# A two-layer Conformer-style trunk: the FFN's feature tiles in parts of 4, 9 and 9 instead of 5, 8 and 9, with two of GpSimd's weight sums in other buffers

## The chip, the cores and the metric

The kernel runs on one core of a Trainium2 chip. The metric is the device time of one execution in microseconds; before the change its median over three runs is 1799.12 us (1798.94 to 1799.37). The engines of the core go by their profile names: PE (TensorE, matrix products), DVE (VectorE), ACT (ScalarE), POOL (GpSimd) and SP (SyncE, which here only issues DMAs). Each engine works through its own queue in order and waits on semaphores for what other engines and DMAs have to finish first.

## The reference

The trunk has two layers on one sequence of 512 positions with 1024 channels. Only the FFNs matter for the change; there are four of them, two in each layer, before and after a mixer of convolution and differential attention.

```python
def swiglu(h, w_gate, w_up, w_down):
    return (jax.nn.silu(h @ w_gate) * (h @ w_up)) @ w_down
...
    for l in range(DEPTH):
        x = x + 0.5 * swiglu(rms_norm(x, ffn1_norm[l]), ffn1_w_gate[l], ffn1_w_up[l], ffn1_w_down[l])
        h = rms_norm(x, mix_norm[l])
...
        x = x + jnp.concatenate([conv_out, diff_out], axis=-1) @ w_out[l]
        x = x + 0.5 * swiglu(rms_norm(x, ffn2_norm[l]), ffn2_w_gate[l], ffn2_w_up[l], ffn2_w_down[l])
```

All of it is float32. `w_gate` and `w_up` are 1024 x 2816, `w_down` is 2816 x 1024. The mixer also needs one scalar lambda per layer (exponentials of two sums of products) and a table of relative-position biases; both depend on small inputs alone and are made once.

## The kernel before

**Products in three parts.** The activation `x` lies in SBUF with channels on the partitions, as 8 tiles of 128 x 512. Each float32 operand of a large product is split into a high part (ACT, L96) and a low part (DVE, L97, the value minus its high part), and a product is three matmuls: high by high, high by low, low by high (L159, L162, L163 in `mm3`). `ring` hands out the buffers for weights: `wraw` has 5 slots of 128 x 1024 for weights as loaded, `whi` and `wlo` have 4 each for the parts.

**FFN.** `ffn` works on the 22 feature tiles (128 features each) in three parts, `PARTS = ((0, 5), (5, 8), (13, 9))`: first tile and number of tiles of each. For each part it makes the gated activations of its tiles (`hh`, `hl`, high and low), then the down projection of this part (`ps_d`, L455 to L463), whose result DVE adds to `x` by one eviction for each of the eight output tiles m (L463). A down projection is three matmuls of 128x512 for each pair of feature tile and m, so 24 per feature tile. `gather` (L103) loads its weights on SP, eight blocks of 128 columns at a time.

There are two ways to make a feature tile's gate and up products:

- Plain tiles, those below `PLAIN`, which is the number of tiles in the first part. Each is 2 x 8 x 3 = 48 matmuls of 128x512 (`products`). DVE and ACT then multiply by the norm's factors, apply SiLU and gate (L441 to L444), and split the result (L407). The norm's factors `r` come from statistics that are made while the first tiles are multiplied, so these products work on unnormalized `x`.
- Seven-product tiles, all others. `seven` treats gate and up as the two halves of one 2 x 2 block product and does it with seven block products in place of eight, each of 4 x 3 matmuls of 128x256: 84 (L367). It needs sums of blocks on both sides. Those of the activation are made once for each FFN, after `r` is known, by `Halves`: DVE normalizes `x` into `hn` (L326), makes the differences in `ht` (L330 to L333), ACT and DVE split these into `th` and `tl` (L335), and `settle` splits `hn` itself into `acth` and `actl` (L341) after the part's last plain product, in the buffers that held the unnormalized parts.

**Sums of weights.** `sums` (L120) makes those of the weights for each seven-product tile. SP loads the gate block (`whole`, one `wraw` slot), halves of gate and up into a second slot (`two`), and a third of 128 x 512 in `wraw2`. A DMA from POOL's queue adds half of the up block to both halves of `two` (L137). POOL then makes two more sums (L142, L143) in a third `wraw` slot, `more`. ACT and DVE split all seven operands.

**PSUM.** `turn_tag` deals three pairs of banks in turn, to each feature tile's two banks (`pair_banks`) and to each two outputs m of a down projection; a bank is reused when whoever read it last is done. `tmp` is a pool of scratch buffers, where the norms keep squares (`sq`, two), their sum (`ssum`, one) and a diagonal (`diag`, one).

**Work on the side.** `aside`, passed to the first FFN of layer 0 alone, calls `make_scalars` (lambda: a load on POOL's queue and products on POOL, L496 and L498; a sum on DVE, L500) and `make_bias` (the bias table: one-hot loads, a small matmul `ps_bias` L480, negation on DVE L481, and DMAs through DRAM on POOL's queue, L477, L482, L484). They are called where the tile loop comes to m = 4. A scheduler orders the instructions of each engine from there on; some matmuls are held to their place in the program by `keep_in_program_order`.

Of the kernel before, what the change touches and what calls it, by code (L numbers as in the profile page):

```python
# [11 lines left out]
F32 = mybir.dt.float32  # L12
# [3 lines left out]
ALU = mybir.AluOpType  # L16
AX = mybir.AxisListType

P = 128
DEPTH = 2  # L20
SEQ = 512
# [4 lines left out]
FT = DFF // P  # L26
# [14 lines left out]
HS = SEQ // 2  # L41


PARTS = ((0, 5), (5, 8), (13, 9))
PLAIN = PARTS[0][1]

SPACE = 392
# [19 lines left out]
def trunk(ctx: ExitStack, tc: tile.TileContext, xt, par, lamv, relb, onehot,  # L67
          gu1, dn1, wag, wqkv, wout, gu2, dn2, out):
    nc = tc.nc
    V, S, G, T = nc.vector, nc.scalar, nc.gpsimd, nc.tensor  # L70
# [5 lines left out]
    tmp = ctx.enter_context(tc.tile_pool(name="tmp", bufs=2))  # L76
# [3 lines left out]
    def f32(ap):  # L80
        return ap.bitcast(F32)
# [9 lines left out]
    def ring(tag, n=1024):  # L91
        dt = F32 if "raw" in tag else F32R
        return wp.tile([P, n], dt, tag=tag, name=tag, bufs=RING[tag])

    def parts_of(raw, hi, lo, eng=None):
        S.activation(hi, raw, AF.Copy)  # L96
        (eng or V).tensor_tensor(out=lo, in0=raw, in1=f32(hi), op=ALU.subtract)  # L97

    def chunk(src, eng=None):
        raw, hi, lo = ring("wraw"), ring("whi"), ring("wlo")  # L100
        nc.sync.dma_start(raw, src)
        parts_of(raw, hi, lo, eng)
        return hi, lo  # L103

    def gather(src, blocks, eng=None):
# [11 lines left out]
        parts_of(raw[:, c], hi[:, c], lo[:, c], eng)  # L117
        return hi, lo

    def sums(g, u):  # L120

        h = slice(0, 512), slice(512, 1024)
        w = {}

        def give(name, t, n, raw):
            w[name] = tuple(p[:, h[n]] for p in t)
            parts_of(raw, *w[name])

        whole = ring("wraw")
        nc.sync.dma_start(whole, g)  # L130
        two = ring("wraw")
        nc.sync.dma_start(two[:, h[0]], g[:, h[0]])
        nc.sync.dma_start(two[:, h[1]], u[:, h[1]])
        u2 = ring("wraw2", 512)
        nc.sync.dma_start(u2, u[:, h[1]])

        nc.gpsimd.dma_start(  # L137
            two.rearrange("p (b c) -> p b c", b=2), u[:, h[0]].unsqueeze(1).broadcast_to([P, 2, 512]), accum_op=ALU.add
        )

        more = ring("wraw")
        G.tensor_tensor(more[:, h[0]], two[:, h[1]], whole[:, h[0]], op=ALU.add)  # L142
        G.tensor_tensor(more[:, h[1]], more[:, h[0]], whole[:, h[1]], op=ALU.add)  # L143
        t = ring("whi"), ring("wlo")
        parts_of(whole, *t)
        for n, name in enumerate(("g1", "g2")):
            w[name] = tuple(p[:, h[n]] for p in t)
        t = ring("whi"), ring("wlo")
        give("u2u1", t, 0, two[:, h[1]])
        give("g1u2u1", t, 1, more[:, h[0]])  # L150
        give("u2", (ring("whi2", 512), ring("wlo2", 512)), 0, u2)
        t = ring("whi"), ring("wlo")
        give("all", t, 0, more[:, h[1]])
        give("g1u1", t, 1, two[:, h[0]])
        return w

# [21 lines left out]
    for half in range(2):  # L178
        h, kk = slice(half * 512, (half + 1) * 512), range(half * KT // 2, (half + 1) * KT // 2)
# [88 lines left out]
    def products(pr, w, ps, i, at=None, amid=None):  # L268

        got = None  # L270
        for k in range(KT):
            if k == at:
                got = amid()
            mm3(ps, wpart(w[i], k), pr[k], k == 0, k == KT - 1, pin=at is not None and k in (0, at))
        return got

    def lead_products(pr, w, ps):

        for k in range(KT):
            for n in range(2):  # L280
                for i in range(2):
                    mm3(ps[n][i], wpart(w[n][i], k), pr[k], k == 0, k == KT - 1)
        return rows_rstd(pr.s, DM, pin=True)[0]

    def first_products(pr, w, ps, early=False):


        if not early:
            rc, v = rows_rstd(pr.s, DM)
            r = spread(rc, "rb", split=True)  # L290
        for k in range(KT):
            if early and k == STATS_AT:
                rc, v = rows_rstd(pr.s, DM, pin=True)
            for i in range(2):
                mm3(ps[0][i], wpart(w[0][i], k), pr[k], k == 0, k == KT - 1, pin=early and k in (0, STATS_AT))
        for i in range(2):
            for k in range(KT):
                if early and i == 0 and k == STATS_AT:
                    r = spread(rc, "rb", pin=True)
                mm3(ps[1][i], wpart(w[1][i], k), pr[k], k == 0, k == KT - 1, pin=early and k in (0, STATS_AT))  # L300
        return rc, v, r
# [4 lines left out]
    def pair_banks(turn):  # L306
        tag = turn_tag(turn)
        return [bank(tag, "ps_pair") for _ in range(2)]
# [88 lines left out]
    def ffn(pr, gu, dn, after, lead=None, aside=None):  # L397
        with tc.tile_pool(name="ffn", bufs=1) as fp:
            r = halves = None
            for m0, many in PARTS:  # L400
                hh, held, late = [], [], []

                def gated(n, us):
                    hi = fp.tile([P, SEQ], F32R, tag=f"hh{n}", name="hh")
                    lo = fp.tile([P, SEQ], F32R, tag=f"hl{n}", name="hl")
                    S.activation(hi, us, AF.Copy)
                    V.tensor_tensor(lo, us, f32(hi), op=ALU.subtract)  # L407
                    hh.append((hi, lo))

                def finish():  # L410
                    if late:
                        n, rest = late.pop()
                        gated(n, rest())

                for mm in range(many):
                    m = m0 + mm
                    if m == 4 and aside:
                        aside()
                    if m >= PLAIN:
                        w = sums(gu[m, 0], gu[m, 1])  # L420
                        late.append((mm, seven(halves, w, pair_banks(m), fp, finish, mm == many - 1)))
                        continue
                    w = lead[m] if lead and m < 2 else [chunk(gu[m, 0]), chunk(gu[m, 1])]
                    held.append((mm, w, pair_banks(m)))
                    if m == 0:
                        continue
                    if m == 1 and lead:
                        rc = lead_products(pr, [h[1] for h in held], [h[2] for h in held])
                        continue
                    if m == 1:  # L430
                        _, _, r = first_products(pr, [h[1] for h in held], [h[2] for h in held])
                    elif r is None:
                        products(pr, w, held[-1][2][0], 0)
                        r = products(pr, w, held[-1][2][1], 1, 3, lambda: spread(rc, "rb", pin=True, split=True))
                    else:
                        for i in range(2):
                            products(pr, w, held[-1][2][i], i)
                    for n, _, ps in held:
                        gs = fp.tile([P, 2, SEQ], F32, tag="gn", name="gs", bufs=2)
                        us = gs[:, 1]  # L440
                        V.tensor_tensor(gs[:, 0], ps[0], r, op=ALU.mult)  # L441
                        S.activation(gs[:, 0], gs[:, 0], AF.Silu)
                        V.tensor_tensor(us, ps[1], r, op=ALU.mult)
                        V.tensor_tensor(us, us, gs[:, 0], op=ALU.mult)  # L444
                        gated(n, us)
                    held = []
                    if not halves:
                        halves = Halves(fp, pr, r)
                finish()
                if m0 == 0:  # L450
                    halves.settle()
                blocks = [divmod(m0 + kk, HALF) for kk in range(many)]
                blocks = [(half, m * HALF + f) for m in range(KT) for half, f in blocks]
                w = None
                for m in range(KT):  # L455

                    ps = bank(turn_tag(m0 + many + m // 2), "ps_d")
                    for kk in range(many):
                        b = m * many + kk
                        if b % 8 == 0:  # L460
                            w = gather(dn, blocks[b : b + 8])
                        mm3(ps, wpart(w, b % 8), hh[kk], kk == 0, kk == many - 1)
                    V.scalar_tensor_tensor(x[:, m, :], ps, 0.5, x[:, m, :], op0=ALU.mult, op1=ALU.add)  # L463
                    if m0 + many == FT:
                        after(m)
# [354 lines left out]
    def aside():  # L820
        make_scalars()
        make_bias()
# [92 lines left out]
```

## Time and profile before

| | |
|---|---|
| median of 3 runs | 1799.12 us (1798.94 to 1799.37) |
| profiled execution, time | 1801.19 us |
| profiled execution, span | 1799.4 us |
| PE busy | 1782.5 us, 99%, 10836 matmuls |
| DVE busy | 1225.8 us, 68%, 1858 instructions |
| ACT busy | 895.1 us, 50% |
| POOL busy | 644.3 us, 36%, 460 instructions |
| granted PE clock | 1.0 |

The span runs from the first to the last instruction of the profiled execution. A busy share is a mean over the whole span, while each stage has its own limit, so the times below are read from windows and timelines of single stages. Matmuls are pipelined and the profile draws each longer than its pitch; the pitch is the distance of two starts. The row of a timeline gives start, duration, engine, line and operation, output and inputs, and in brackets how long the engine had been idle and what ended that. Rows with a count of x2 or more are several instructions in succession.

### The profile page before, as it was taken

The numbers are of one execution on the slowest core, as the hardware profiler recorded it, in microseconds if no ns is written. First come the engines' busy times: TensorE is split into PE (matmuls) and PEld (weight loads), VectorE is DVE, ScalarE is ACT, GpSimd is POOL, SyncE is SP. The second block draws the span as 40 slices with busy tenths as digits, with TensorE's granted clock in tenths as the row PEclk, the third lists the DMA queues.
The fourth block names the chain that finished last, engine by engine and source line by source line (L and its number), as shares of the span: only waits on it lengthen the run. The fifth ranks groups of instructions, "written<-read, shape, count | busy, mean of one in ns | idle before, by whom it ended". The sixth has DMA issues, their size and how long they took to land.

```text
span 1799.4 us, 28320 instructions
## 1 busy us (share of the span) xinstructions
PE 1782.5 (99%) x10836; PEld 1588.6 (88%) x10836; DVE 1225.8 (68%) x1858; ACT 895.1 (50%) x1478; POOL 644.3 (36%) x460
## 2 busy tenths in 40 slices
PE   8999999999999999999999999999999999999999
PEld 6899899888778899899888998998887888998997
DVE  7966477568867867477567764765788587674762
ACT  5555255445854446256333653654558354552651
POOL 4242132269943132133112422312797332322320
PEclk9999999999999999999999999999999999999999
DMA  7366467333212266466333654663231133664651
GB/s 242 104 177 187 103 162 199 105 106 93 71 44 87 85 165 184 115 166 183 115 96 94 170 170 108 187 181 118 70 108 57 48 103 92 164 181 112 181 148 59
DMA packets 111145, 231.24 MB, mean 129 GB/s; under 512 B 12087, under 2 KB 32326, under 8 KB 111008
## 3 DMA queue, kind: packets, MB, share of 16 engines
q1 hardware_dynamic: 90912, 191.93, 32.8%
q0 software_dynamic: 19808, 37.33, 12.4%
q8 instruction: 85, 1.39, 0.3%
q14 instruction: 52, 0.43, 0.1%
q10 hardware_dynamic: 288, 0.16, 0.0%
HBM read 227.26 MB, written 3.42 MB: 128 GB/s over the span
## 4 chain that ended last, share of the span: by engine, by line
PE 92%; DVE 2%; DMA 2%; issue 1%; ACT 1%; POOL 0%; POOLq 0%; SPq 0%; ACTq 0%; DVEq 0%
PE ps_pair L367 35%; PE ps_d L163 9%; PE ps_d L162 9%; PE ps_d L159 9%; PE ps_pair L163 5%; PE ps_pair L162 5%; PE ps_pair L159 5%; DMA wraw<-in_gu 2%; PE ps_pair L581 2%; PE ps_pair L580 2%; PE ps_pair L579 2%; PE ps_sc L697 2%; PE ps_out L162 1%; PE ps_out L163 1%; PE ps_out L159 1%
## 5 line engine op out<-in xcount | busy, mean ns | idle before, releaser
L96 ACT ACTIVATE whi<-wraw 128x512 fp32r<-128x512 f32 (+1 forms) x596 | 466.0, 805 | 618.5 <-PE ps_pair L367 213.5
L97 DVE TENSOR_TENSOR wlo<-wraw,whi 128x512 fp32r<-128x512 f32 (+1 forms) x552 | 540.6, 1001 | 206.3 <-ACT whi L96 201.5
L367 PE MATMUL ps_pair<-acth,wlo 128*128 128x256 f32 x1088 | 308.1, 283 | 1.6 <-DVE wlo L97 1.6
L367 PE MATMUL ps_pair<-acth,whi 128*128 128x256 f32 x1088 | 307.9, 283 | 0.3 <-ACT whi L96 0.3
L367 PE MATMUL ps_pair<-actl,whi 128*128 128x256 f32 x1088 | 307.9, 283 | 0.0
L162 PE MATMUL ps_d<-hl,whi 128*128 128x512 f32 x704 | 273.9, 389 | 0.0
L163 PE MATMUL ps_d<-hh,wlo 128*128 128x512 f32 x704 | 273.0, 389 | 0.0
L159 PE MATMUL ps_d<-hh,whi 128*128 128x512 f32 x704 | 268.4, 389 | 0.0
L367 PE MATMUL ps_pair<-th,wlo 128*128 128x256 f32 x816 | 230.9, 283 | 0.0
L367 PE MATMUL ps_pair<-tl,whi 128*128 128x256 f32 x816 | 230.8, 283 | 0.0
L367 PE MATMUL ps_pair<-th,whi 128*128 128x256 f32 x816 | 230.8, 283 | 0.0
L137 POOL DMA_DIRECT2D wraw<-in_gu x68 | 82.0, 1206 | 408.0 <-DMA wraw<-in_gu 241.1
L142 POOL TENSOR_TENSOR wraw<-wraw 128x512 f32<-128x512 f32 x68 | 102.4, 1506 | 336.7 <-DMA wraw<-in_gu 285.1
L367 PEld LDWEIGHTS ps_pair<-acth,wlo 128*128 128x128 f32 x1088 | 208.8, 192 | 2.0 <-DVE wlo L97 2.0
L367 PEld LDWEIGHTS ps_pair<-acth,whi 128*128 128x128 f32 x1088 | 208.8, 192 | 0.8 <-ACT whi L96 0.5
L367 PEld LDWEIGHTS ps_pair<-actl,whi 128*128 128x128 f32 x1088 | 208.8, 192 | 0.3
L463 DVE SCALAR_TENSOR_TENSOR x<-ps_d,x 128x512 f32<-128x512 f32 x96 | 64.7, 689 | 177.9 <-PE ps_d L163 177.5
L159 PE MATMUL ps_pair<-acth,whi 128*128 128x512 f32 x448 | 175.3, 395 | 5.6 <-ACT whi L96 5.6
L162 PE MATMUL ps_pair<-actl,whi 128*128 128x512 f32 x448 | 175.7, 393 | 0.3 <-DVE actl L252 0.2
L163 PE MATMUL ps_pair<-acth,wlo 128*128 128x512 f32 x448 | 174.9, 391 | 0.5 <-DVE wlo L97 0.5
L367 PEld LDWEIGHTS ps_pair<-tl,whi 128*128 128x128 f32 x816 | 156.5, 192 | 0.7
L367 PEld LDWEIGHTS ps_pair<-th,whi 128*128 128x128 f32 x816 | 156.5, 192 | 0.6
(172 smaller groups left out, 3253.4 us busy)
## 6 DMA issues: line engine op xcount, KB each, us to landing
wraw<-in_gu SPq DMA_DIRECT2D x212, 256.0 KB, 3.9
wraw<-in_gu SPq DMA_DIRECT2D x104, 512.0 KB, 3.6
wraw<-in_gu POOLq DMA_DIRECT2D x68, 512.0 KB, 5.6
wraw<-in_wqkv SPq DMA_DIRECT2D x24, 512.0 KB, 3.6
wraw<-in_dn SPq DMA_DIRECT2D x84, 128.0 KB, 2.8
wraw<-in_dn SPq DMA_DIRECT2D x32, 256.0 KB, 2.9
wraw<-in_wag SPq DMA_DIRECT2D x16, 512.0 KB, 3.5
wraw<-in_wout SPq DMA_DIRECT2D x16, 512.0 KB, 3.5
```

The lines of the kernel that those rows point to most:

```text
L96: S.activation(hi, raw, AF.Copy)
L97: (eng or V).tensor_tensor(out=lo, in0=raw, in1=f32(hi), op=ALU.subtract)
L137: nc.gpsimd.dma_start(two.rearrange("p (b c) -> p b c", b=2), u[:, h[0]].unsqueeze(1).broadcast_to([P, 2, 512]), accum_op=ALU.add)
L142: G.tensor_tensor(more[:, h[0]], two[:, h[1]], whole[:, h[0]], op=ALU.add)
L159: first = T.matmul(ps, wh, xh, start=start, stop=False)
L162: T.matmul(ps, wh, xl, start=False, stop=False)
L163: T.matmul(ps, wl, xh, start=False, stop=stop)
L367: mm = T.matmul(ps, l, r, start=first and i == j == 0, stop=False, skip_group_check=True)
L463: V.scalar_tensor_tensor(x[:, m, :], ps, 0.5, x[:, m, :], op0=ALU.mult, op1=ALU.add)
L579: T.matmul(ps[n], xh[:, t], wh, start=k == 0, stop=False)
L580: T.matmul(ps[n], xh[:, t], wl, start=False, stop=False)
L581: T.matmul(ps[n], xl[:, t], wh, start=False, stop=k == KT - 1)
```

## The change

Three things change. `PARTS` becomes `((0, 4), (4, 9), (13, 9))`, so tile 4 of every FFN turns from a plain into a seven-product tile, the first down projection covers four feature tiles and the second nine. The two sums that POOL makes in `sums` go from one `wraw` slot into two scratch buffers of 128 x 512 of the pool `tmp`: `three` in the tag `sq`, `four` by turns in `diag` and `ssum`. And `aside` is called at m = 3. Lines of the changed kernel below L118 stand two to three lines further down.

```diff
-PARTS = ((0, 5), (5, 8), (13, 9))
+PARTS = ((0, 4), (4, 9), (13, 9))
 PLAIN = PARTS[0][1]
...
+    count = iter(range(DEPTH * 2 * FT))
+
     def sums(g, u):
...
-        more = ring("wraw")
-        G.tensor_tensor(more[:, h[0]], two[:, h[1]], whole[:, h[0]], op=ALU.add)
-        G.tensor_tensor(more[:, h[1]], more[:, h[0]], whole[:, h[1]], op=ALU.add)
+        three = tmp.tile([P, SEQ], F32, tag="sq", name="three")
+        four = tmp.tile([P, SEQ], F32, tag=("diag", "ssum")[next(count) % 2], name="four", bufs=1)
+        G.tensor_tensor(three, two[:, h[1]], whole[:, h[0]], op=ALU.add)
+        G.tensor_tensor(four, three, whole[:, h[1]], op=ALU.add)
...
-        give("g1u2u1", t, 1, more[:, h[0]])
+        give("g1u2u1", t, 1, three)
...
-        give("all", t, 0, more[:, h[1]])
+        give("all", t, 0, four)
...
-                    if m == 4 and aside:
+                    if m == 3 and aside:
                         aside()
```

## The prediction, made before the changed kernel was run

> **What bounds the kernel now.** I read the profile page first: span, engine totals, chain of waits.
>
> ```profile
> span 1799.4 us, 28320 instructions
> ...
> PE 1782.5 (99%) x10836; PEld 1588.6 (88%) x10836; DVE 1225.8 (68%) x1858; ACT 895.1 (50%) x1478; POOL 644.3 (36%) x460
> ...
> PE 92%; DVE 2%; DMA 2%; issue 1%; ACT 1%; POOL 0%; POOLq 0%; SPq 0%; ACTq 0%; DVEq 0%
> ```
>
> TensorE works through 99% of the span and 92% of the chain that ended last. Two things can move the time: how many TensorE cycles the products take, and where TensorE stands still. For the first I read windows in which nothing but one kind of matmul runs (us; then each engine's busy time with its count in brackets).
>
> ```profile
> 765.00:805.00 40.00, 40.00 (x336) 40.00 (x334) 28.72 (x39) 23.45 (x42) 13.70 (x10) 1.00 0.60 153
> 1207.00:1247.00 40.00, 40.00 (x178) 33.11 (x177) 22.12 (x26) 17.22 (x23) 7.40 (x5) 1.00 0.33 106
> ```
>
> 336 matmuls of 128x256 in 40 us are 0.119 us each; 178 of 128x512 are 0.225. Some records can be missing, so I check the second with the timeline of the first down projection, whose 120 matmuls stand between the starts of these two rows:
>
> ```profile
> 66.03 0.39 PE L159 MATMUL ps_d<-hh,whi 128*128 128x512 f32 x1
> ...
> 93.23 0.28 PE L367 MATMUL ps_pair<-acth,whi 128*128 128x256 f32 x1
> ```
>
> 27.20 / 120 = 0.2267 us. The second row also shows the place on which most of this depends: the boundary at which the plain tiles and their down projection end and the seven-product tiles begin, in the first FFN of layer 0. There is no gap at it now. What keeps it closed is VectorE's slack, so I read VectorE's timeline there (start, duration, instruction; in brackets the idle time before and who ended it).
>
> ```profile
> 37.66 1.23 DVE L97 TENSOR_TENSOR wlo<-wraw,whi 128x1024 fp32r<-128x1024 f32 x1
> 39.95 0.69 DVE L441 TENSOR_TENSOR gs<-ps_pair,rb 128x512 f32<-128x512 f32 x1 [1.06 <-ACT rb L238]
> 40.56 0.68 DVE L443 TENSOR_TENSOR gs<-ps_pair,rb 128x512 f32<-128x512 f32 x1
> ...
> 49.79 1.20 DVE L97 TENSOR_TENSOR wlo<-wraw,whi 128x1024 fp32r<-128x1024 f32 x1
> 50.92 0.74 DVE L330 TENSOR_TENSOR ht<-hn 128x256 f32<-128x256 f32 x2
> ...
> 54.90 0.29 DVE L500 TENSOR_REDUCE lamd<-lamv 128x2 f32<-128x128 f32 x1 [0.50 <-POOL lamv L498]
> ...
> 76.89 1.81 DVE L335 TENSOR_TENSOR tl<-ht,th 128x768 fp32r<-128x768 f32 x2
> 81.65 1.89 DVE L463 SCALAR_TENSOR_TENSOR x<-ps_d,x 128x512 f32<-128x512 f32 x3 [2.95 <-PE ps_d L163]
> 83.45 1.58 DVE L97 TENSOR_TENSOR wlo<-wraw,whi 128x1024 fp32r<-128x1024 f32 x1
> ...
> 93.43 0.69 DVE L463 SCALAR_TENSOR_TENSOR x<-ps_d,x 128x512 f32<-128x512 f32 x1 [2.26 <-PE ps_d L163]
> ```
>
> From 39.95 VectorE works without a pause, but for 0.50 at 54.90, until 78.70 (76.89 + 1.81): the gated activations, the norm's halves and their sums for the seven products, the weight splits. Then it waits 2.95 us for TensorE before the first eviction of the down projection (L463). Spacing of two neighbours: 0.60 per 128x512 operation (39.95, 40.56; also evictions, 1.80 for three from 81.65 to 83.45), 1.13 per split of a 128x1024 weight (49.79, 50.92). Slack here is 2.95 us and what lies between the evictions.
>
> **The change, part by part.**
>
> *One tile more by seven products.* In each FFN 48 matmuls of 512 become 84 of 256: 48 x 0.2267 = 10.88 against 84 x 0.119 = 10.00, or 10.79 with the window's 0.2247. I take 0.8 us saved, 3.2 over four FFNs (bounds 0.79 and 0.88, 3.2 to 3.5). The down matmuls stay 528 per FFN; 24 move from the first part to the third and cost the same there. The tile's extra elementwise work on VectorE, ScalarE and GpSimd lies under 10 us of matmuls, as that of the other seven-product tiles does: the 765 window has VectorE busy 28.72 of 40 us, GpSimd 13.70.
>
> *The first boundary, layer 0.* TensorE now reaches it earlier by one plain tile and 24 down matmuls: 10.88 + 5.44 = 16.32, so at 93.23 - 16.32 = 76.9 if nothing stops it. Does VectorE get there? The order of its instructions up to 55.44 is the one of before. The first seven-product tile opens with the product of `u2u1`, whose PSUM bank is that of the down projection's output m=6; it can't start before VectorE has evicted this bank, and the next product needs m=7. In VectorE's new order both stand behind everything: all halves of the norm (`tl` last), six evictions, the split of the tile's first weight and four splits of 128x512. The groups of the window 39.9 to 78.7 say what falls out:
>
> ```profile
> L97 DVE TENSOR_TENSOR wlo<-wraw,whi 128x1024 fp32r<-128x1024 f32 x5 | 6.0, 1205 | 0.0
> ...
> L441 DVE TENSOR_TENSOR gs<-ps_pair,rb 128x512 f32<-128x512 f32 x5 | 3.4, 682 | 1.1 <-ACT rb L238 1.1
> L407 DVE TENSOR_TENSOR hl<-gs,hh 128x512 fp32r<-128x512 f32 x5 | 3.4, 673 | 0.0
> L444 DVE TENSOR_TENSOR gs<-gs 128x512 f32<-128x512 f32 x5 | 3.3, 675 | 0.0
> ```
>
> One of the five pairs goes: one each of L441, L443, L407, L444, 4 x 0.60 = 2.4 us. Of the five 1024-wide splits three stay in this stretch: 2 x 1.13 = 2.26 less. Added behind, up to the eviction of m=7: eight evictions 4.8, the weight split 1.13, four splits 4 x 0.60 = 2.4. So 78.70 - 2.4 - 2.26 + 4.8 + 1.13 + 2.4 = 82.4 for m=7 and 81.8 for m=6, and TensorE, ready at 76.9, begins at 81.8: a new stall of 4.9 us. It is the same work in the order of arrival, now without the cover of the fifth pair.
>
> Two terms lengthen this chain. The lambda work is called at the fourth pair in place of the fifth, and GpSimd's queue gets the accumulating DMA of the first seven-product tile (L137) ahead of the second one-hot load (L477), the second lambda load (L496) and the DMA of the bias row. GpSimd now:
>
> ```profile
> 44.07 1.25 POOL L498 TENSOR_TENSOR lamv<-lamv 128x64 f32<-128x64 f32 x2 [4.14 <-DMA lamv<-in_lamv]
> 45.28 0.54 POOL L477 DMA_DIRECT2D oneh<-in_onehot  x1
> 48.97 0.57 POOL L496 DMA_DIRECT2D lamv<-in_lamv  x1 [3.15 <-DVE lamd L500]
> ...
> 52.25 2.61 POOL L498 TENSOR_TENSOR lamv<-lamv 128x64 f32<-128x64 f32 x2 [1.59 <-DMA lamv<-in_lamv]
> ...
> 64.00 1.28 POOL L137 DMA_DIRECT2D wraw<-in_gu  x1 [2.16 <-DVE actl L341]
> 81.27 1.29 POOL L142 TENSOR_TENSOR wraw<-wraw 128x512 f32<-128x512 f32 x1 [15.99 <-DMA wraw<-in_gu]
> 82.64 1.30 POOL L143 TENSOR_TENSOR wraw<-wraw 128x512 f32<-128x512 f32 x1
> ```
>
> The tile's raw weights come through SP once the split at 37.66 has freed their slot, so the accumulation can go at 45.3, when L498 ends, takes 1.2 to issue, and the loads follow at about 46.5 and 48.97. VectorE's second lambda sum already waits for L498 (0.50 at 54.90), so whatever the lambda load lands later than now, 52.25, counts in full. Bounds: 0.3, if only the queue's issue is passed on, and 1.0, if a transfer of 4.5 us from 46.5 (the 4.53 below) holds it until 51 and it then needs about its 2.2 us; I take 0.4, since both can move at once. Its four sums of 128x512 now fall in the stretch in which VectorE is full. The row at 83.45 is a split of 1.58 us instead of 1.20, with GpSimd's sum of 82.64 running over its beginning: 0.38 per meeting; 0 to 4 x 0.6 = 2.4 for four meetings (twice a 0.60 operation). I take two of them, 0.8. Together 4.9 + 0.4 + 0.8 = 6.1 us, bounds 5.2 (4.9 + 0.3 + 0) and 8.3 (4.9 + 1.0 + 2.4).
>
> *The other three boundaries.* Layer 0's second FFN, VectorE:
>
> ```profile
> 618.80 0.69 DVE L407 TENSOR_TENSOR hl<-gs,hh 128x512 fp32r<-128x512 f32 x1
> 625.17 1.89 DVE L463 SCALAR_TENSOR_TENSOR x<-ps_d,x 128x512 f32<-128x512 f32 x3 [5.68 <-PE ps_d L163]
> ...
> 640.81 0.69 DVE L463 SCALAR_TENSOR_TENSOR x<-ps_d,x 128x512 f32<-128x512 f32 x1 [2.71 <-PE ps_d L163]
> ```
>
> It is free at 619.49 and waits 5.68. By the same sum, with one split less in the stretch: 619.49 - 2.4 - 1.13 + 8.33 = 624.3 for m=7, 623.7 for m=6, against a TensorE that comes at 640.6 - 16.3 = 624.3. No cover is left, no debt either. The rows of layer 1 look the same. I take 0.4 each, 1.2 in all (0 to 2.5): a sum of GpSimd that is late holds the splits in VectorE's queue, and the evictions behind them.
>
> *GpSimd's sums in scratch buffers.* TensorE's only stops inside a seven-product stage stand in part three of that first FFN:
>
> ```profile
> 247.40 0.39 PE L367 MATMUL ps_pair<-acth,wlo 128*128 128x256 f32 x1 [0.78 <-DVE wlo L97]
> ...
> 288.07 0.39 PE L367 MATMUL ps_pair<-acth,whi 128*128 128x256 f32 x1 [0.30 <-ACT whi L96]
> ...
> 289.42 0.39 PE L367 MATMUL ps_pair<-acth,wlo 128*128 128x256 f32 x1 [0.84 <-DVE wlo L97]
> ```
>
> 0.78 + 0.30 + 0.84 = 1.92 us idle. A matmul that follows at a pitch of 0.119 is drawn 0.28 long, and the stalled ones 0.39, so each stop is 0.16 + 0.11 longer than the idle column says: 2.7 us. GpSimd at these places:
>
> ```profile
> 236.89 1.20 POOL L137 DMA_DIRECT2D wraw<-in_gu  x1 [7.30 <-DMA wraw<-in_gu]
> 245.52 1.28 POOL L142 TENSOR_TENSOR wraw<-wraw 128x512 f32<-128x512 f32 x1 [7.42 <-DMA wraw<-in_gu]
> ...
> 254.16 1.30 POOL L142 TENSOR_TENSOR wraw<-wraw 128x512 f32<-128x512 f32 x1 [4.53 <-DMA wraw<-in_gu]
> ...
> 277.99 1.20 POOL L137 DMA_DIRECT2D wraw<-in_gu  x1 [0.65 <-DVE wlo L97]
> 287.55 1.26 POOL L142 TENSOR_TENSOR wraw<-wraw 128x512 f32<-128x512 f32 x1 [8.35 <-DMA wraw<-in_gu]
> ```
>
> Its sums wait 7.42 and 8.35 us for the accumulated weights where 4.53 is usual, and the accumulations themselves waited for loads or splits. The `wraw` ring has five slots and a tile takes three; with the sums elsewhere two. Look-ahead goes from 5/3 to 5/2 tiles, 0.83 x 10.0 = 8.3 us, against lateness of 8.35 - 4.53 = 3.8. I take all 2.7 off (bounds 0 and 2.7). The scratch buffers themselves belong to the norm, which isn't running there; a wait for them I cost at nothing, since GpSimd is busy 13.70 of 40 us.
>
> Sum: -3.2 - 2.7 + 6.1 + 1.2 = +1.4 us. The profiled execution took 1801.19 (span 1799.4 and 1.8 around it), so it would take 1802.6; it lies 2.1 over the median of 1799.12, and against that median the forecast is 1800.5.
>
> **Rivals.**
>
> (a) *The cover suffices.* ScalarE and VectorE run the splits and evictions as TensorE delivers and no boundary opens: -3.2 - 2.7 = -5.9, 1793.2. For it: the 2.95 us of slack; against it: the sum above, in which 16.3 us of cover meet 4.7 us of work that falls out.
>
> (b) *The stops of part three stay.* If the long landings come from full DMA queues and not from late slots, 2.7 us aren't won: 1803.2, slower. For it: 7.42 and 8.35 are waits after the issue; against it: no other seven-product stage stops.
>
> (c) *GpSimd's queue decides; slower.* The accumulation ahead of the lambda load takes the 8.35 us of the 277.99 row in place of 4.5: it lands at 46.5 + 8.35 = 54.9, the lambda load 0.5 to 2.2 behind it, and L498 (2.61) ends at 58.0 to 59.7 instead of 54.90. VectorE stands in front of its second lambda sum, with every half, eviction and split of the boundary behind it: 3.1 to 4.8 us, less the 0.4 counted, so 1803.2 to 1804.9, say 1804.3. It decides from a landing of the lambda load after 53.5. For it: the row of 64.00, whose accumulation needed 16 us and more at the head of this stage; against it: that one stood behind the large bias DMA, which now comes later.
>
> (d) *Each GpSimd sum shuts VectorE out for its whole length.* 4 x 1.30 = 5.2 in place of 0.8, 1804.9. Against it, here GpSimd was the loser:
>
> ```profile
> 615.14 5.50 POOL L142 TENSOR_TENSOR wraw<-wraw 128x512 f32<-128x512 f32 x1 [4.47 <-DMA wraw<-in_gu]
> ```
>
> A sum of 1.3 us took 5.50 while VectorE ran back to back to 619.49. The Trainium skill (page "SBUF — State Buffer", section "Who interferes with whom") says that a VectorE instruction with two SBUF inputs and a GpSimd instruction that reads SBUF share one port pair, which the first to start holds for the whole instruction. By that rule either can lose; the trace agrees with both, 1.58 for 1.20 at 83.45 and 5.50 for 1.3 here.
>
> **How the numbers follow.** Chances: forecast 0.56 (its own range, with the stops of part three gone: -3.5 - 2.7 + 5.2 + 0 gives 1798.1, -3.2 - 2.7 + 8.3 + 2.5 gives 1804.0), (a) 0.11, (b) 0.09, (c) 0.17, (d) 0.07. 0.2% of 1799.12 is 3.6 us, about what a measurement of this kernel can tell from no change. Faster, under 1795.5: (a) and 0.01 for a forecast that misses its bounds, 0.12. Slower, over 1802.7: 0.09 of the forecast, 0.05 of (b), 0.13 of (c), 0.05 of (d), 0.32. Same: 0.56. The range of 8 in 10 leaves out (a) and the upper ends of (c) and (d) with a dearer boundary: 1795.0 to 1806.5.
>
> **What would show it.** Right: a gap of TensorE of 4 to 8 us ahead of the first seven-product tile at 77 to 84 us, ended by VectorE's eviction of `ps_d`; no idle TensorE between 200 and 290; the seven-product tile still 10.0 us; gaps under 1 us at the other three boundaries. Wrong: TensorE at that tile by 78 (a); stops of 1 us in part three with GpSimd waiting over 7 us (b); VectorE idle for more than 1.5 us before L500, ended by L498 (c); splits over 2 us between 55 and 82 (d); or a gap at a place not named here, a norm's scratch buffer first of all.

## The result and the profile after

The changed kernel takes 1807.92 us (median of 4 runs, 1806.93 to 1809.21) against 1799.03 for the kernel before (4 runs): 8.9 us more, ratio 1.005 with a 95% interval of 1.0039 to 1.0062. The forecast was 1800.5 with a range to 1806.5. It is slower, by 7.4 us more than forecast.

The page of the changed kernel, the lines that answer to those of before:

```profile
span 1806.2 us, 28722 instructions
...
PE 1782.1 (99%) x10980; PEld 1594.6 (88%) x10980; DVE 1242.5 (69%) x1878; ACT 908.0 (50%) x1506; POOL 663.5 (37%) x472
...
PE 91%; DVE 5%; issue 1%; ACT 1%; POOL 0%; DVEq 0%; ACTq 0%; POOLq 0%
```

TensorE's busy total is the same and its share is still 99%, so the totals alone hide the loss. The view of what TensorE waits for (total, times, longest, in us) names it:

```profile
PE ps_pair L370 <- DVE x L466: 5.0, 4, 3.8
...
PE ps_d L162 <- ACT hh L409: 1.8, 1, 1.8
PE ps_d L162 <- DVE gs L444: 1.6, 1, 1.6
```

None of these three stood there before, and the waits for weight splits in part three (1.6 and 0.3) are gone. TensorE's timeline says where they are:

```profile
60.10 0.50 PE L162 MATMUL ps_d<-hh,whi 128*128 128x512 f32 x1 [1.56 <-DVE gs L444]
...
67.64 0.73 PE L162 MATMUL ps_d<-hh,whi 128*128 128x512 f32 x2 [1.80 <-ACT hh L409]
...
85.34 0.55 PE L370 MATMUL ps_pair<-acth,whi 128*128 128x256 f32 x1 [3.80 <-DVE x L466]
...
632.38 0.36 PE L370 MATMUL ps_pair<-acth,whi 128*128 128x256 f32 x1 [0.63 <-DVE x L466]
```

By start to start the first three gaps are 1.72, 1.96 and 3.96 longer than the pitch, 7.65 us together, all in the first FFN of layer 0; at the other boundaries 0.79 (the last row), 0.46 and 0.46. Then the windows around the first seven-product tile, whose column behind the POOL count is the granted TensorE clock:

```profile
85.30:91.50 6.20, 6.16 (x29) 6.19 (x30) 1.84 (x3) 1.01 (x2) 1.10 (x1) 0.50 0.87 195
91.50:95.00 3.50, 3.50 (x31) 3.50 (x31) 0.88 (x2) 1.67 (x3) 0.87 (x1) 1.00 0.60 184
```

29 matmuls in 6.2 us at a clock of 0.50, then 31 in 3.5 us at 1.00: after the longest gap 27 matmuls come at a pitch of 0.214 instead of 0.120 us. That is 2.5 us which no step of the forecast had.

VectorE's timeline at this boundary, and GpSimd's:

```profile
55.43 0.29 DVE L503 TENSOR_REDUCE lamd<-lamv 128x2 f32<-128x128 f32 x1 [0.50 <-POOL lamv L501]
...
55.96 3.49 DVE L344 TENSOR_TENSOR actl<-hn,acth 128x512 fp32r<-128x512 f32 x2
...
64.37 1.27 DVE L344 TENSOR_TENSOR actl<-hn,acth 128x512 fp32r<-128x512 f32 x2
...
76.75 1.64 DVE L338 TENSOR_TENSOR tl<-ht,th 128x768 fp32r<-128x768 f32 x1
...
81.24 0.94 DVE L338 TENSOR_TENSOR tl<-ht,th 128x768 fp32r<-128x768 f32 x1
...
84.52 1.27 DVE L466 SCALAR_TENSOR_TENSOR x<-ps_d,x 128x512 f32<-128x512 f32 x2
```

```profile
55.68 1.52 POOL L145 TENSOR_TENSOR three<-wraw 128x512 f32<-128x512 f32 x1 [0.29 <-PE ps_bias L483]
57.28 1.62 POOL L146 TENSOR_TENSOR four<-three,wraw 128x512 f32<-128x512 f32 x1
...
66.59 9.60 POOL L145 TENSOR_TENSOR three<-wraw 128x512 f32<-128x512 f32 x1
76.27 1.29 POOL L146 TENSOR_TENSOR four<-three,wraw 128x512 f32<-128x512 f32 x1
```

Lambda's second sum (55.43) still waits only 0.50 for GpSimd, so the new queue order cost nothing there. But two splits (L344) took 3.49 us from 55.96 where two take 1.27 at 64.37, while GpSimd made its first pair of sums (55.68 to 58.90); the third `tl` took 1.64 where the fourth took 0.94, while the sum of 76.27 ran. GpSimd's sum of 66.59 took 9.60 us instead of 1.3. The evictions of m = 6 and 7 end at 85.79, not at 82.4.

To add up, a stop-free profile of the kernel before (the run e_before_again below, 1798.86 us) is the better partner. First matmul behind the first FFN, and last matmul of the kernel, in its timeline and in that of the changed kernel:

```profile
357.60 0.39 PE L159 MATMUL ps_pair<-acth,whi 128*128 128x512 f32 x1
...
1792.77 0.39 PE L163 MATMUL ps_d<-hh,wlo 128*128 128x512 f32 x1
```

```profile
367.52 0.39 PE L162 MATMUL ps_pair<-acth,whi 128*128 128x512 f32 x1
...
1801.89 0.39 PE L166 MATMUL ps_d<-hh,wlo 128*128 128x512 f32 x1
```

The first FFN ends 9.92 us later (0.29 of it because TensorE began so much later; 7.65 + 2.5 - 0.8 explains 9.35) and the rest takes 1434.37 instead of 1435.17, 0.80 less. All of the loss is made in the first FFN.

### The profile page after: what moved, and what is told of

The parts are those of the page before. It is cut to its first block, busy times and chain, and to the rows that moved or that the text cites. A ratio compares the mean times of both kernels' runs of the same rounds, so it can differ in the third digit from the quotient of the medians.

```text
span 1806.2 us, 28722 instructions
## 1 busy us (share of the span) xinstructions
PE 1782.1 (99%) x10980; PEld 1594.6 (88%) x10980; DVE 1242.5 (69%) x1878; ACT 908.0 (50%) x1506; POOL 663.5 (37%) x472
## 4 chain that ended last, share of the span: by engine, by line
PE 91%; DVE 5%; issue 1%; ACT 1%; POOL 0%; DVEq 0%; ACTq 0%; POOLq 0%
PE ps_pair L370 40%; PE ps_d L162 8%; PE ps_d L165 8%; PE ps_d L166 8%; PE ps_pair L166 4%; PE ps_pair L165 4%; PE ps_pair L162 4%; PE ps_pair L584 2%; PE ps_pair L582 2%; PE ps_pair L583 2%; DVE wlo L97 1%; PE ps_out L165 1%; PE ps_out L162 1%; PE ps_sc L700 1%; PE ps_out L166 1%
## 5 line engine op out<-in xcount | busy, mean ns | idle before, releaser
L96 ACT ACTIVATE whi<-wraw 128x1024 fp32r<-128x1024 f32 (+1 forms) x468 | 396.3, 851 | 487.0 <-PE ps_d L165 179.9
L97 DVE TENSOR_TENSOR wlo<-wraw,whi 128x512 fp32r<-128x512 f32 (+1 forms) x424 | 447.3, 1057 | 185.2 <-ACT whi L96 180.9
L370 PE MATMUL ps_pair<-acth,whi 128*128 128x256 f32 x1152 | 327.1, 284 | 5.0 <-DVE x L466 5.0
L370 PE MATMUL ps_pair<-actl,whi 128*128 128x256 f32 x1152 | 326.7, 284 | 0.0
L370 PE MATMUL ps_pair<-acth,wlo 128*128 128x256 f32 x1152 | 326.7, 284 | 0.0
L145 POOL TENSOR_TENSOR three<-wraw 128x512 f32<-128x512 f32 x72 | 114.8, 1595 | 421.2 <-DVE wlo L97 182.3
L139 POOL DMA_DIRECT2D wraw<-in_gu x72 | 86.5, 1202 | 305.6 <-DMA wraw<-in_gu 195.7
L370 PEld LDWEIGHTS ps_pair<-th,wlo 128*128 128x128 f32 x864 | 166.3, 192 | 0.0
L162 PEld LDWEIGHTS ps_d<-hh,whi 128*128 128x128 f32 x704 | 132.1, 188 | 31.0 <-ACT hh L409 2.2
L162 PE MATMUL ps_pair<-acth,whi 128*128 128x512 f32 x384 | 150.2, 395 | 6.3 <-ACT whi L96 6.3
L166 PEld LDWEIGHTS ps_d<-hh,wlo 128*128 128x128 f32 x704 | 132.2, 188 | 27.1
```

The lines of the kernel that those rows point to most:

```text
L139: nc.gpsimd.dma_start(two.rearrange("p (b c) -> p b c", b=2), u[:, h[0]].unsqueeze(1).broadcast_to([P, 2, 512]), accum_op=ALU.add)
L145: G.tensor_tensor(three, two[:, h[1]], whole[:, h[0]], op=ALU.add)
L162: first = T.matmul(ps, wh, xh, start=start, stop=False)
L166: T.matmul(ps, wl, xh, start=False, stop=stop)
L370: mm = T.matmul(ps, l, r, start=first and i == j == 0, stop=False, skip_group_check=True)
```

## The experiments

Times are medians of 4 to 11 runs, each beside runs of the kernel before on the same chip (1798.79 to 1798.90).

**The half clock.** Twelve matmuls fill most of the longest gap:

```diff
+                if m0 == 0 and aside:
+                    idle = bank("tp", "ps_idle")
+                    for n in range(12):
+                        mm = T.matmul(idle, hh[0][0][:, :P], hh[1][0], start=True, stop=True)
+                        tc.keep_in_program_order(mm)
```

> The changed kernel with twelve matmuls of 128x512 (2.7 us) into a free PSUM bank, unread, between the first down projection and the first seven-product tile of the first FFN, so that TensorE idles about 1.2 us there instead of 3.9. Theory C, the half clock that follows (0.50 for 6.1 us) comes from the idle time: the tile starts at the same moment but at a pitch of 0.12, 2.8 us won, 1805.1. Rival, the clock falls for another reason (or the profile only draws it so): 1807.9.

> The changed kernel, unchanged: 1807.9 within 1; the half clock after the first boundary again, if it belongs to the program and not to one execution.

Measured: 1805.64 us with the matmuls, 1807.21 without; in the profiles 1803.6 and 1806.1 of span. TensorE and the windows with the matmuls:

```profile
82.69 2.88 PE L472 MATMUL ps_idle<-hh 128*128 128x512 f32 x12
85.41 0.28 PE L370 MATMUL ps_pair<-acth,whi 128*128 128x256 f32 x1
```

```profile
85.40:91.50 6.10, 6.10 (x52) 6.09 (x51) 1.89 (x3) 1.87 (x4) 0.72 (x1) 1.00 0.92 207
```

The tile starts at 85.41, as late as without them (85.34), with 52 matmuls in 6.1 us in place of 29 and a clock of 1.00. So the half clock comes from TensorE's standing still. The matmuls keep the clock up behind this gap alone: in the same execution the gap that ends at 67.32, 1.79 us long, was followed by a clock of 0.50 from 68.5 to 71.9. That moved nothing, since the tile waits for VectorE all the same. The half clock isn't worth a fixed sum: the repeated profile of the changed kernel lost 2.2 us by it (23 matmuls), the first one 2.5, and the medians give 1.6. In all nine executions of the changed kernel the mean granted clock is 0.998 or 0.999: the three with 0.999 took 1806.67 to 1806.93 us and the six with 0.998 took 1807.21 to 1809.21.

**Undoing the parts one by one.** The scratch buffers alone on the kernel before; the ring's slot back in the changed kernel; the call at m = 3 alone; the kernel before once more.

```diff
-PARTS = ((0, 4), (4, 9), (13, 9))
+PARTS = ((0, 5), (5, 8), (13, 9))
...
-                    if m == 3 and aside:
+                    if m == 4 and aside:
```

> The kernel before with the scratch buffers alone (parts 5, 8, 9; lambda work at the fifth pair). Theory A, the stops of part three that the profile of before shows (2.7 us) hardly exist in unprofiled runs, which fits a profiled execution 2.1 us over the median: time 1799.0 within 0.6, and a profile without those stops whose own time is near its median. Theory B, they are in every run: 1796.3.

> The kernel before, unchanged: ratio 1.000. Theory A: its profile shows stops in part three of another length than 2.7 us, and its own time is over the median by about as much. Theory B: the same stops, and a time over the median that has nothing to do with them.

> The changed kernel with GpSimd's two sums back in a slot of the wraw ring. Theory A: within 1 us of the changed kernel, 1807 to 1809, since the scratch buffers are worth nothing in time. Theory B: 2.7 dearer, 1810.6, with stops of 1 us in part three again.

> The kernel before with the lambda and bias work called at m = 3, nothing else. VectorE's slack of 2.95 us covers it: 1799.0 within 0.5. If the earlier call itself costs, through GpSimd's queue: 1800 and more.

Measured: the kernel before again 1799.02, and its profile has no stop in part three (the window 260 to 300: TensorE busy throughout, 336 matmuls).

```profile
260.00:300.00 40.00, 40.00 (x336) 40.00 (x335) 30.85 (x44) 24.62 (x44) 16.30 (x11) 1.00 0.70 184
```

That profiled execution took 1798.86, the one the forecast was made from 1801.19 with 2.7 us of stops. So they belonged to that execution and not to the median: theory A on this point. The early lambda call alone is 1798.79: nothing. The scratch buffers alone are 1801.29, 2.4 slower, where A had no difference and B a gain; both were wrong. With the ring's slot back the changed kernel is at 1808.32, and the half clock has moved: it stands behind the gap of 1.80 us inside the down projection (first row, and the window after it). So TensorE reaches the tile later, and the last gap is only 2.04 us, with the clock up behind it (34 matmuls in the next 4 us). The other three boundaries open to 1.74 each.

```profile
67.21 2.67 PE L161 MATMUL ps_d<-hh,whi 128*128 128x512 f32 x6 [1.80 <-ACT hh L408]
...
84.76 0.36 PE L369 MATMUL ps_pair<-acth,whi 128*128 128x256 f32 x1 [2.04 <-DVE x L465]
```

```profile
67.60:70.90 3.30, 3.30 (x9) 2.62 (x8) 3.30 (x6) 1.63 (x3) 1.26 (x1) 0.50 0.34 117
```

Where the scratch buffers lose, in the order of TensorE, GpSimd and SP's queue in the run e_scratch:

```profile
154.46 0.39 PE L370 MATMUL ps_pair<-acth,wlo 128*128 128x256 f32 x1 [0.68 <-DVE wlo L97]
```

```profile
108.20 2.16 POOL L146 TENSOR_TENSOR four<-three,wraw 128x512 f32<-128x512 f32 x1
110.31 1.19 POOL L139 DMA_DIRECT2D wraw<-in_gu  x1
118.50 1.80 POOL L145 TENSOR_TENSOR three<-wraw 128x512 f32<-128x512 f32 x1 [7.01 <-DVE ps_pair L393]
```

```profile
110.38 0.33 SPq L134 DMA_DIRECT2D wraw<-in_gu  x1
110.76 0.42 SPq L135 DMA_DIRECT2D wraw<-in_gu  x1
```

TensorE stops three times, all in part two of the first FFN (143.45, 154.46, 165.24), for splits that come late. GpSimd issues the accumulating DMA (L139) at 110.31, right behind its last sum, and its next sum starts 8.19 us later. At 110.38 and 110.76 SP issues the two loads of the next tile's `two`: their slot was the earlier `whole`, whose last reader is this same sum. Both transfers fly together. Over all tiles the median from the accumulation's issue to the next sum is 7.2 us with the scratch buffers (over 7 in 37 of 68), against 6.0 in the stop-free run of the kernel before (4 of 68). It is the DMA itself that got longer, and not a wait for the scratch buffers: the pages give its median time from issue to landing, first the stop-free run of the kernel before, then e_scratch:

```profile
wraw<-in_gu POOLq DMA_DIRECT2D x68, 512.0 KB, 5.8
...
wraw<-in_gu POOLq DMA_DIRECT2D x68, 512.0 KB, 7.1
```

In this part GpSimd's round becomes 11.4 us against 10.0, and TensorE's tile takes 10.1. GpSimd's rounds are as slow in the other three FFNs (medians of 10.8 to 12.0), yet TensorE doesn't stop there. The long waits that the profile of before showed fit: at 236.89 it issues an accumulation that took 8.63, and SP's queue there reads

```profile
238.27 0.33 SPq L132 DMA_DIRECT2D wraw<-in_gu  x1
238.65 0.47 SPq L133 DMA_DIRECT2D wraw<-in_gu  x1
```

Two tries to undo this alone failed. Each adds a third `wraw` slot per tile that a copy of eight columns touches, on GpSimd ahead of or behind the accumulation:

```diff
+        spare = ring("wraw")
+        G.tensor_copy(spare[:, :8], u2[:, :8])
...
+        G.tensor_copy(spare[:, :8], two[:, 512:520])
```

> The kernel before with the scratch buffers, and beside them a third wraw slot for each seven-product tile that only a copy of eight columns touches, so that the ring turns as before. Theory F: what costs 2.3 us in the run with the scratch buffers alone is the turn of the ring. With two slots a tile, the loads of `two` wait for GpSimd's last sum, after which GpSimd also issues the next accumulation, so both fly together and the accumulation needs 7 us in place of 4.6; GpSimd's round grows to 11.5 us against TensorE's 10.1. Then this kernel has waits of 4.6 to 5, no stops in part two, and 1799.0. Rival: the sums are slower into the scratch buffers, or wait for them; then 1801.3.

> The kernel before with the scratch buffers and a third wraw slot a tile, touched by a copy of eight columns that now waits for the accumulation as GpSimd's first sum did before (in the earlier such run the copy stood ahead of the accumulation and held GpSimd's queue). Theory F, the turn of the ring costs the 2.3 us: the time from the accumulation's issue to GpSimd's next operation is 5.8 to 6.0 us as before and not 7.2, no stops in part two, 1799.0 within 0.6. Rival, the scratch buffers themselves: 1801.3.

Measured: 1808.31 and 1875.59. In both, SP's next loads came only behind the copy (in the first a copy at 122.20 and loads from 122.89, in the second 146.41 and 146.62), and the next accumulation went out well after these loads (129.65 and 153.52). So the time of neither kernel speaks for or against theory F. Their pages do speak for its first half: with the scratch buffers in use but three slots a tile, the accumulation's median landing is back at 5.8 and 5.7 us. That the longer landing is also what costs the 2.4 us rests on the alignment of the rows and on no clean undoing.

**What VectorE waits on at the boundary.** Without GpSimd's first four sums, and with the lambda and bias work moved behind the boundary:

```diff
+        if bare:
+            three, four = whole[:, h[0]], whole[:, h[1]]
...
-                    if m == 3 and aside:
+                    if m == 8 and aside:
```

> The changed kernel without GpSimd's two sums in the first two seven-product tiles of the first FFN (their products use two weights as loaded instead, so the output is not the reference's). Theory E, these sums held VectorE for about 3.0 us (one pair of splits took 3.49 instead of 1.27, one split of the halves 1.64 instead of 0.87): the tile starts 3 us earlier, the clock stays up, 5.9 won, 1802.0. Rival, VectorE is slow there for another reason: 1807.9.

> The changed kernel with the lambda and bias work called at m = 8, behind the first boundary. Theory D, the boundary is VectorE's chain and each operation of it counts: 0.2 + 0.2 + 0.5 idle + 0.6 + 0.2 + 0.14 = 1.85 us come off, the idle of TensorE ahead of the first seven-product tile falls to about 2 us and the clock stays: 1.85 + 2.9 = 4.7 won, 1803.2. Rival, GpSimd's queue order with this work is the whole loss: 1794 to 1797. If the clock falls all the same: 1806.

Measured: 1805.91 without the sums (1802.62 to 1809.60). The tile starts at 82.38 instead of 85.16 in the repeated profile, 2.8 us earlier, as theory E has it (3.0):

```profile
65.38 1.66 PE L166 MATMUL ps_d<-hh,whi 128*128 128x512 f32 x6 [1.47 <-ACT hh L413]
...
82.38 0.36 PE L374 MATMUL ps_pair<-acth,whi 128*128 128x256 f32 x1 [3.10 <-DVE x L470]
```

But 3.10 us idle were still enough for a half clock (0.60 in the 4 us that follow), and stops of part two came in, so the median gained 1.3 and not 5.9. With the lambda work late it is 1813.51, 6.3 over the changed kernel on the same chip:

```profile
80.60 0.55 PE L370 MATMUL ps_pair<-acth,whi 128*128 128x256 f32 x1 [3.82 <-DVE x L466]
...
115.58 0.38 PE L483 MATMUL ps_bias<-oneh,relb 33*4 33x128 f32 x2 [2.09 <-DVE nlam L507]
```

The tile starts at 80.60, 4.6 us earlier. VectorE's chain, from its first gated product to the tile, is 4.2 us shorter than in the first profile of the changed kernel (39.96 to 80.60 against 40.46 to 85.34): the 1.85 expected, and two splits of `actl` that take 1.28 here and took 3.49 there. But TensorE also comes earlier (its down projection begins at 53.46 instead of 55.36 and one of its two gaps is gone), so the last gap stays at 3.82 and the clock falls. Then `ps_bias`, held to its place in TensorE's queue, stops the seven-product tiles (115.58, 2.09), and a late weight does so at 149.69 (2.07); behind each of these two the clock is 0.50 for 3.3 us more. The rival, that GpSimd's queue order with this work is the whole loss, falls: with this work moved behind the boundary the last gap is as long as before.

**Where the loss is, and a way round it.** The first FFN in parts of 5, 8 and 9 and the rest in 4, 9 and 9, with the scratch buffers everywhere or with the ring's slot in the first FFN; then the last two outputs of the first part (m = 6 and 7) in the banks of m = 2 and 3, in the last three FFNs or in all four of the changed kernel.

```diff
+            parts = ((0, 5), (5, 8), (13, 9)) if aside else PARTS
+            for m0, many in parts:
...
-                    ps = bank(turn_tag(m0 + many + m // 2), "ps_d")
+                    ps = bank(turn_tag(m0 + many + ((0, 1, 2, 1) if m0 == 0 and not aside else (0, 1, 2, 3))[m // 2]), "ps_d")
```

> Parts 4, 9, 9 in the last three FFNs only; the first keeps 5, 8, 9 and its lambda work at the fifth pair; sums in the scratch buffers. If the loss lies at the first boundary alone: three times -0.8 for the products and +1.25 for the gaps that the changed profile shows at the other boundaries, so 1797.9 by theory A and 1795.2 by theory B. If the other three FFNs carry part of the loss: over 1799.

> First FFN as before (5, 8, 9, sums in the ring, lambda work at the fifth pair), the other three 4, 9, 9 with the scratch buffers. Three times -0.8, and gaps of 0.46 to 0.80 at three boundaries (1.7): 1798.3 within 0.5. If the scratch buffers cost in these FFNs too: 1800 or more.

> The run before this one (e_mix), with the outputs m = 6 and 7 of the first part's down projection in the banks of m = 2 and 3 in the last three FFNs, so that the first seven-product tile opens in the banks of m = 0 and 1, evicted long before. If the gaps at these boundaries are waits for the eviction of m = 6: 1.7 less, 1796.6. If the splits behind them are late too: 1798.

> The changed kernel with m = 6 and 7 of every first part's down projection in the banks of m = 2 and 3. The first boundary then waits for the split of u2u1 and not for the evictions behind four splits: about 2.5 us earlier, the idle time under 2 us, so the clock stays up (2.4 to 2.9 more), and 1.25 to 2.0 at the other boundaries: 1801.0 within 1. If VectorE's work ahead of it, not the order behind it, sets the whole stall: 1806.

Measured: e_first5 1800.41 (1798.10 to 1803.51, with a stop of part two in its profile, as with the scratch buffers alone), e_mix 1798.41, e_rot 1796.86, e_rotall 1801.00. The three later boundaries of e_mix:

```profile
622.70 0.35 PE L374 MATMUL ps_pair<-acth,whi 128*128 128x256 f32 x1 [0.63 <-DVE x L471]
...
968.93 0.36 PE L374 MATMUL ps_pair<-acth,whi 128*128 128x256 f32 x1 [0.30 <-DVE x L471]
...
1513.35 0.35 PE L374 MATMUL ps_pair<-acth,whi 128*128 128x256 f32 x1 [0.62 <-DVE x L471]
```

And the first of them in e_rot, where the last matmul of the down projection and the first of the tile are 0.22 apart:

```profile
622.11 0.39 PE L170 MATMUL ps_d<-hh,wlo 128*128 128x512 f32 x1
622.33 0.28 PE L374 MATMUL ps_pair<-acth,whi 128*128 128x256 f32 x1
```

The gaps were waits for the eviction of m = 6 behind the tile's splits, and the exchange of banks takes them all: e_rot has a ratio of 0.9987 (0.9978 to 0.9996) to the kernel before, 1.9 us less, and beats both. In the changed kernel the same exchange wins 6 to 7 us. At the first boundary three short gaps are left, and in the profiled execution no half clock follows:

```profile
59.81 0.50 PE L162 MATMUL ps_d<-hh,whi 128*128 128x512 f32 x1 [1.56 <-DVE gs L444]
...
67.34 1.66 PE L162 MATMUL ps_d<-hh,whi 128*128 128x512 f32 x6 [1.79 <-ACT hh L409]
...
76.58 0.50 PE L162 MATMUL ps_d<-hh,whi 128*128 128x512 f32 x1 [0.76 <-DVE x L466]
```

4.6 us of gaps against 7.65: so about 3 us of the stall were the order in which the evictions stood behind the splits. The 4.6 that stay I put down to VectorE's work ahead of the evictions; no run undoes that alone.

## Why the prediction was wrong, by its own steps

- **48 matmuls to 84, 0.8 us per FFN:** right. e_mix keeps three of the four changed FFNs: -2.4 and gaps of 2.0 (0.79, 0.46 and 0.78 over the pitch) make -0.4, measured 1798.41 against 1798.79, -0.4. (The 24 down matmuls go to the second part, not to the third as the prediction says; its sum doesn't depend on it.)
- **The first boundary, 6.1 us (5.2 to 8.3):** VectorE's chain sets it, as forecast, but the size was small, 7.65, and the place half wrong. The forecast let TensorE run through to 76.9 and put the whole stall ahead of the tile. TensorE stops twice inside the down projection (1.72 and 1.96), for a bank that VectorE has still to read (L444) and for the last pair's `hh`; 3.96 stand where the forecast had all of it. The chain itself was worked out at 4.9, and without GpSimd's sums the gaps are 4.9 (1.63 and 3.26). What was mis-sized is GpSimd's meeting with VectorE, 0.8 in the sum, about 2.8 by that run. That is rival (d) half way: two sums shut VectorE out, and in the other meeting GpSimd lost 8.3 us. The row quoted for it (1.58 for 1.20) was a meeting of short overlap. The 0.4 for lambda wasn't spent.
- **A stall costs its length:** the step that the forecast took for granted, and it failed. After 3.8 us of idle TensorE ran at half clock and lost 2.2 to 2.5 us more. The profile of before has no idle of this length inside a stage, but it has one at the kernel's start, and its rows show what follows:

```profile
5.62 0.79 PE L159 MATMUL ps_pair<-acth,whi 128*128 128x512 f32 x1 [5.62 <-ACT whi L96]
...
8.07 0.63 PE L159 MATMUL ps_pair<-acth,whi 128*128 128x512 f32 x1
8.50 0.63 PE L162 MATMUL ps_pair<-actl,whi 128*128 128x512 f32 x1
```

  Matmuls of 128x512 start 0.43 us apart here in place of 0.2267, as they do in the window of e_ring at a clock of 0.50. (The clock column reads 1.00 at this place, so only the pitch tells.) The Trainium skill (page "TensorE: Matmul & The Clock Gate", section "🔬 Part 1: The HAM clock gate (the "warmup" mystery)") says that TensorE's clock drops to half after an idle window of about 3.4 us and rises after as long a busy one. The trace agrees on the drop, but not on the length: idle of 3.10, 3.80 and 3.82 us was followed by half clock, and so was idle of 1.79 (e_warm), 1.80 (e_ring) and 2.09 (e_late), while 1.80 in the changed kernel and 2.04 in e_ring were not. The length of one gap doesn't decide it alone; what does stays open. A rival by this rule belonged in the forecast, since its own gap lay at 4.9 us.
- **The other three boundaries, 1.2 us (0 to 2.5):** right in size, 1.7, and the evictions do stand behind the splits, as e_rot shows. But no late sum of GpSimd holds these splits. At the first of the three VectorE works without a pause up to the eviction of m = 6 at 631.56, and two splits of `tl` take 2.91 us (621.59) in place of 1.81 while GpSimd makes its sums.
- **The stops of part three, -2.7:** wrong. They were in one profiled execution, whose time lay 2.1 us over the median; I carried this difference over to the median and also took the stops off it. The scratch buffers, meant here as look-ahead, slow GpSimd's round, and alone cost 2.4 us. In the changed kernel no stop shows, probably because the late first boundary gives GpSimd a lead: without the four sums the boundary comes 2.8 us earlier, and part two stops again.
- **Rivals:** (a) fell, since the stall came; (b) was nearer in its effect, though for another reason; (c) fell, with lambda's wait at 0.50 as before; (d) half right.

The terms that failed: stall 7.65 for 6.1, 1.55; half clock 2.5 for 0; stops 0 for -2.7; other boundaries 1.7 for 1.2. Together 7.25 over the forecast, measured 7.4.

## What to carry to other kernels

Ahead of adding up gains from a profile, set that execution's time against the median: a loss that is in the one and not in the other can't be won. Where a change moves TensorE ahead of an engine with a full queue, work out each gap and not only their sum, because a gap can be followed by half clock: here every one of 3.1 us and more was, and some of about 2. Look at which buffer the first instruction behind a boundary needs: here the gain of a cheaper product (0.4 us of 2.4 left) only became one worth having when that instruction no longer stood behind an eviction (1.6 us more).

## What the runs showed of the hardware

- TensorE's granted clock went to 0.50 after idle gaps of 3.1 us and more, and after some of 1.8 to 2.1 us but not others of the same length. It stayed there for 3 to 6 us. Twelve unread matmuls in the longest gap kept it at 1.00 behind that gap.
- A GpSimd sum of 128x512 and VectorE's splits of SBUF tensors hold each other up both ways: two splits took 3.49 instead of 1.27 us, and a sum 9.60 instead of 1.3 under VectorE's unbroken work.
- An accumulating DMA of 512 KB from GpSimd's queue landed after 7.1 us (median) in the run where two loads from SP's queue were issued right behind it, against 5.8 in the stop-free run of the kernel before. That the loads are the cause is argued from the rows, not shown.
